# Where the gate columns and the key columns of the retention group stand in a diffusion layer's order of stages

## The chip, the cores and the metric

The kernel runs on 1 core of one Trainium2 chip. The metric is device time in microseconds (us) of one execution, lower is better. A core has five engines, each with a queue of its own that it works off in the order in which the program put it there: TensorE (PE, matrix products; the profile shows its weight loads apart as PEld), VectorE (DVE), ScalarE (ACT), GpSimd (POOL) and SyncE (SP, which here only issues transfers). ACT and POOL issue transfers too.

## The reference, cut to what matters

One layer over 1024 latent tokens and 256 context tokens of width 1024. All tokens go through one input projection, whose columns feed two groups of four heads: a gated delta rule (A) and retention (B).

```python
p = concat([h_ctx, h_lat]) @ w_in                       # 1280 x 4112
qkv_a, z, ab, rq, rk, rv, rg = split(p)                 # 1536, 512, 16, 512, 512, 512, 512 columns
q, k, v = split(short_conv(qkv_a))                      # A: 5 taps along the tokens, then silu
q, k = l2_normalize(q) * HEAD_DIM ** -0.5, l2_normalize(k)
o_gdn = rms_norm(o_f + o_b) * silu(z)                   # o_f, o_b: gated_delta_rule, both directions
rq, rk = apply_rope(rq), apply_rope(rk) * HEAD_DIM ** -0.5
o_ret = head_group_norm(r_f + r_b) * silu(rg)           # r_f, r_b: retention, both directions
y = concat([o_gdn, o_ret])
x = x + g1 * (y @ w_out)
x = x + g2 * swiglu(modulate(rms_norm(x), sh2, sc2))    # 1024 -> 2 x 2816 -> 1024
```

The delta rule needs, for each chunk of tokens and each direction, the inverse of a triangular matrix made from k; then a scan runs over the chunks. The retention is a second scan, which needs rq, rk and rv of a chunk.

## The kernel before, in words

Every large product is made from split float32 values: an operand x becomes hi (rounded by ACT, L319) and lo = x - hi (DVE or POOL, L320), and hi*hi + hi*lo + lo*hi are three matmuls.

- **Norm and modulation** (up to L309) leave the activations of all 1280 tokens in SBUF as `hhi` and `hlo`, transposed, where they stay until the last projection is done.
- **`token_major(g, tiles, finish, store, pl, q)`** (L371) projects 256 columns: group g of the weights is loaded and split in two halves, then each tile of 128 tokens takes 24 matmuls of 256 columns into a PSUM bank `tm` (three banks), `finish` takes the bank to the tile `res`, and `store`'s queue writes `res` to memory. Groups 0 and 1 are rv, 2 and 3 rk, 4 and 5 rq, 6 and 7 rg (the gate), 8 and 9 z. rv and rk run over 10 tiles, the others over 8. `finish` is one ACT instruction for rv, rg and z; for rk and rq it is `fin_rope` (L393): `ra` (L398) and two halves of `res` (L401) on DVE, two POOL instructions (L403), and the store (L391) on POOL's queue, with two buffers of `res`.
- **`conv_block(b, y, lat)`** (L475) projects 128 columns of q, k or v of the delta rule for all tokens (PSUM tile `b2`, `b` in the profile), runs the five taps (ACT L488, DVE L494) and the silu. For k, `kstat` transposes it and makes scales; `ada_rest` puts a column block of the conditioning on DVE (L336) beside it.
- **`pre(t)`** (L568) prepares chunk t of 128 tokens: k times k (`kk`), the transposed q (`qt`), k times q (`kq`), all in three PSUM banks of tag `pb` that are taken in turn; then for each direction the decay matrix `e` from a loaded row `gw` (POOL L591, L593, ACT L595), the tile `ut` (DVE L603), and for latent chunks `sp` (DVE L605, ACT L608, POOL L609). Two buffers each of `gw`, `e`, `ut`, `sp`.
- **`invert(b)`** (L616) inverts 32 x 32 blocks of a batch of chunks by 31 pairs of small DVE instructions (`tmp`, `X`: L638, L640), **`merge(b)`** (L664) puts the blocks together (PE tiles `m`), through the tile `U`, of which there is one buffer. The batches are [0,1,2,9], [3,8,4,7] and [5,6].
- **The scans**: `step(s, d)` (L766; matmuls kS, Tr, up, o) is one step of the delta rule in direction d. `rstate` (L884; matmul `ru`) and `forward` are the retention. A small chain of constants (`rdl`, `lg`, `Z`, from L857) stands ahead of the first `ru`; its tiles lie where `hhi` lay, so it begins once the last projection is done.
- Output projection, feed-forward and final norm follow; they begin at about 720 us of the span.

The code is written in the order norm, rv, k convolutions, q convolutions, rg, chunks of batches 0 and 1 with their inversions, v convolutions, chunks of batch 2, merges, z, first two scan steps, rk, rq, the rest of the scans. This order is only a priority. A scheduler that orders by its own cost estimate fixes each engine's queue when the kernel is built: where it thinks that the next instruction of a higher priority isn't ready, it puts a later one there. So matmuls of a projection stand between those of other stages as filling. On the chip the queues are worked off in that fixed order.

A pool's memory is reused tile by tile: `pre`'s tiles (pool `gp`) lie where the pools `w2` and `r2` were, which `token_major` for rg and `ada_rest` used.

Of the kernel before, what the change touches and what calls it, by code (L numbers as in the profile page):

```python
# [8 lines left out]
F32 = mybir.dt.float32  # L9
# [8 lines left out]
P = 128  # L18
# [5 lines left out]
TT = NTOK // P  # L24
# [13 lines left out]
def build(nc, tc, ap, dbg=None, stop=None, marks=None):  # L38
    root = ExitStack()
    V, S, G, T, SY = nc.vector, nc.scalar, nc.gpsimd, nc.tensor, nc.sync  # L40

    def pool(name, bufs=1, side=None, space=None):
        kw = {}
        if side is not None:
            kw["side"] = side
        if space is not None:
            kw["space"] = space
        if space is not DRAM:
            kw["reuse_waits"] = "tile"
        es = ExitStack()  # L50
        p = es.enter_context(tc.tile_pool(name=name, bufs=bufs, **kw))
        root.push(es)
        p_close[id(p)] = es
        return p
# [3 lines left out]
    def close(p):  # L58
        p_close.pop(id(p)).close()
# [5 lines left out]
    def checkpoint(name):  # L65
        if dbg is not None:
            marks.append((name, int(nc.cur_bb.bb.instructions[-1].name.split("-")[-1])))
        if stop == name:
            raise Stop()
# [91 lines left out]
    try:  # L161
# [13 lines left out]
        W = pool("w", bufs=2)  # L175
# [79 lines left out]
        W2 = pool("w2", bufs=2)  # L255
# [69 lines left out]
        def ada_rest(c, half):  # L325

            c0 = c * D + half * 512
            acc = R2.tile([P, 512], F32, tag="acc", name="acc", bufs=1)
            for k in range(KT):
                if k % 2 == 0:  # L330
                    w = R2.tile([P, 2, 512], F32, tag="adaw2", name="adaw2", bufs=2)
                    SY.dma_start(w, ap["ada_w"][k * P:(k + 2) * P, c0:c0 + 512].rearrange("(a p) n -> p a n", p=P))
                if k == 0:
                    V.tensor_scalar(acc, w[:, 0], csl[:, k, 0:1], None, ALU.mult)
                else:
                    V.scalar_tensor_tensor(acc, w[:, k % 2], csl[:, k, 0:1], acc, ALU.mult, ALU.add)  # L336
            ps = bank_b("gr")
            if c in (2, 5):
                row = R2.tile([1, 512], F32, tag="row", name="row", bufs=1)
                SY.dma_start(row, ap["adarow"][c0:c0 + 512].unsqueeze(0))  # L340
                T.matmul(ps[:1, :], ones[:, 0:1], acc, start=True, stop=True)
                V.tensor_tensor(row, row, ps[:1, :], ALU.add)
                SY.dma_start(grow[0 if c == 2 else 1][:, half * 512:(half + 1) * 512], row)
            else:
                for k in range(4):
                    T.matmul(ps[:, 2 * k:2 * k + 2], acc[:, k * P:(k + 1) * P], ones[:, 0:2], start=True, stop=True)
                ks = slice(half * 4, half * 4 + 4)
                o = ada2[:, c - 3, ks]
                V.tensor_tensor(o, ps[:, 0:8].rearrange("p (k t) -> p k t", t=2)[:, :, 0],
                                adab[:, 8 * c + 4 * half:8 * c + 4 * half + 4], ALU.add)  # L350
                if c == 4:
                    V.scalar_tensor_tensor(o, o, 1.0, gffn[:, ks], ALU.add, ALU.mult)
# [18 lines left out]
        def token_major(g, tiles, finish, store, pl, q=S):  # L371

            w = [weights(ap["wt"][g, :, 4 * kh:4 * kh + 4, :], [4, 256], V, pl, q, raws.get((g, kh)), g == 0)
                 for kh in range(2)]
            c0 = (g % 2) * 256
            for t in tiles:
                tsl = slice(t * P, (t + 1) * P)
                o = bank_a("tm")[:, 0:WIDE if g == 0 else 256]
                for k in range(KT):
                    whi, wlo = w[k // 4]  # L380
                    T.matmul(o, hhi[:, k, tsl], whi[:, k % 4, :], start=(k == 0), stop=False)  # L381
                    T.matmul(o, hhi[:, k, tsl], wlo[:, k % 4, :], start=False, stop=False)  # L382
                    T.matmul(o, hlo[:, k, tsl], whi[:, k % 4, :], start=False, stop=(k == KT - 1))  # L383
                early = pl is W2 or g == 0
                res = (W2 if early else R1).tile([P, 256], F32, tag="res", name="res", bufs=4 if early else 2)
                finish(t, o[:, 0:256], res)
                if g == 0:
                    S.activation(xa[:, t, :], o[:, 256:WIDE], AF.Copy)
                nm = GROUPS[g // 2]
                dst = zd[t - 2, :, c0:c0 + 256] if nm == "z" else rd[t, :, RD[nm], c0:c0 + 256]  # L390
                store.dma_start(dst, res)  # L391
# [19 lines left out]
        LAT, ALL = list(range(2, TT)), list(range(2, TT)) + [0, 1]  # L411
        for g in range(2):
            token_major(g, ALL, fin_copy, S, W if g == 0 else W2)
            ada_rest(2, g)
        checkpoint("rv")


# [52 lines left out]
        V.tensor_copy(gT, ps[:80, :P])  # L470
        SY.dma_start(grow_d, gT)
        close(AB)
        CV = pool("cv", side="right")

        def conv_block(b, y, lat):  # L475

            whi, wlo = weights(ap["wg"][b], [KT, P], G if b % 2 else V, W, SY if b in (4, 5) else S)
            u = CV.tile([P, NTOK], F32, tag="u", name="u", bufs=2)
            for c0, n in (CHUNKS[1:] if lat else CHUNKS):
# [19 lines left out]
        def newy():  # L499
            return CV.tile([P, NTOK], F32, tag="y", name="y", bufs=3)  # L500

# [43 lines left out]
        for h in range(H):  # L545
            y = newy()
            conv_block(h, y, True)
            if h < 2:
                ada_rest(5, h)
            S.dma_start(qd[:, :, h, :].rearrange("t p j -> p t j"),  # L550
                        y[:, NCTX:].rearrange("p (t j) -> p t j", j=P))

        checkpoint("q")
        for g in (6, 7):
            token_major(g, LAT, fin_gate, S, W2, SY)
        checkpoint("rg")
        close(R2)
        close(W2)
        GP = pool("gp")
# [153 lines left out]
        def solve(b):  # L713
            for t in BATCH[b]:
                pre(t)
            checkpoint("pre%d" % b)
            invert(b)
            checkpoint("inv%d" % b)

        solve(0)  # L720
        solve(1)
        for h in range(H):
            y = newy()
            conv_block(8 + h, y, False)
            for t0, n in ((0, 2), (2, 4), (6, 4)):
                ps = bank_b("vT")
                for t in range(t0, t0 + n):
                    T.transpose(ps[:, (t - t0) * P:(t - t0 + 1) * P], y[:, t * P:(t + 1) * P], ident)
                vt = CV.tile([P, 4, P], F32, tag="vt", name="vt", bufs=1)
                for t in range(n):  # L730
                    S.activation(vt[:, t], ps[:, t * P:(t + 1) * P], AF.Copy, scale=sv3[:, t0 + t, h:h + 1])
                S.dma_start(vd[t0:t0 + n, :, h, :].rearrange("t p j -> p t j"), vt[:, :n])
        close(CV)
        checkpoint("v")
        RP = pool("rp", side="right")
        rope = RP.tile([P, TT, P], F32, tag="rope", name="rope")
        GM = pool("gm")
        for t in BATCH[2]:
            pre(t)
        checkpoint("pre2")  # L740
        merge(0)
        SY.dma_start(rope, ap["rope"])
        invert(2)
        checkpoint("inv2")
        merge(1)
# [97 lines left out]
        for s in range(NS0):  # L843
            steps(s)
        checkpoint("scan0")
        for g in (2, 3):
            token_major(g, ALL, fin_rope, G, W)
        for g in (4, 5):
            token_major(g, LAT, fin_rope, G, W)
        close(R1)  # L850
# [118 lines left out]
        close(SC)  # L969
        close(RP)  # L970
        close(GS)
# [524 lines left out]
```

## Time and profile before

| What | Value |
|---|---|
| Device time, median of 3 runs | 1504.32 us (1503.76 to 1508.56) |
| The profiled execution | 1499.94 us; its span, from the first to the last instruction, is 1498.2 us |
| Mean granted TensorE clock | 0.974 of full speed |
| Busy in the span | PE 1405.7 us (94%), DVE 978.5 us (65%), POOL 638.6 us (43%), ACT 607.0 us (41%) |
| Chain that ended last | PE 64%, DVE 12%, DMA 10%, POOL 5%, issue 4%, ACT 3% |

Busy time of an engine is the time in which at least one of its instructions ran. A wait is put down to the instruction that ended it. The rows of the trace name a line of the kernel, an engine, an operation, output<-input, a count, then busy time, mean duration in ns, and the idle time of the engine just ahead of them with what ended it.

### The profile page before, as it was taken

How to read it: one execution, taken by the hardware profiler on the slowest of the kernel's cores; microseconds unless marked ns; L12 is line 12 of the kernel's file. 1: busy time of each engine (PE TensorE's matmuls, PEld its weight loads, DVE VectorE, ACT ScalarE, POOL GpSimd, SP SyncE). 2: the span in 40 equal slices, each digit the busy share in tenths (PEclk: the TensorE clock that was granted, in tenths of full speed). 3: DMA queues.
4: the chain of work that ended last, by engine and by line, in shares of the span. 5: the costliest groups of instructions: out<-in, count | busy, mean ns of one | idle time of the engine just before them, and what ended most of it. 6: DMA issues, size and time to landing. Idle time of an engine off the chain costs nothing.

```text
span 1498.2 us, 24215 instructions
## 1 busy us (share of the span) xinstructions
PE 1405.7 (94%) x8927; PEld 1210.8 (81%) x8927; DVE 978.5 (65%) x1926; ACT 607.0 (41%) x1267; POOL 638.6 (43%) x589
## 2 busy tenths in 40 slices
PE   6899999987898899998799899989999999999997
PEld 2898888976888899988678688878888888788886
DVE  5966695279778345678767786646555555658477
ACT  5733653365451121235544433223333333445445
POOL 0310101387124243224326578989555553325322
PEclk9899999997999999999999999999999999999999
DMA  8555685478597756985742256665222231785863
GB/s 329 197 175 164 207 239 167 143 234 267 147 276 213 227 170 252 370 334 204 246 147 106 86 191 223 240 238 204 105 106 106 106 141 68 237 281 188 295 217 113
DMA packets 171703, 298.16 MB, mean 199 GB/s; under 512 B 43368, under 2 KB 93752, under 8 KB 166208
## 3 DMA queue, kind: packets, MB, share of 16 engines
q1 hardware_dynamic: 119424, 251.07, 48.9%
q10 hardware_dynamic: 49360, 36.88, 8.0%
q0 software_dynamic: 2800, 8.65, 1.6%
q8 instruction: 70, 1.15, 0.3%
q14 instruction: 49, 0.40, 0.1%
HBM read 206.60 MB, written 89.96 MB: 198 GB/s over the span
## 4 chain that ended last, share of the span: by engine, by line
PE 64%; DVE 12%; DMA 10%; POOL 5%; issue 4%; ACT 3%; SPq 1%; ACTq 0%; POOLq 0%; DVEq 0%
PE ffn L1187 8%; PE ffn L1186 8%; PE ffn L1185 8%; PE tm L383 4%; PE tm L382 4%; PE tm L381 4%; PE fo L1313 3%; PE fo L1312 3%; PE fo L1311 3%; PE b L484 2%; PE b L486 2%; PE b L485 2%; PE op L1044 2%; PE op L1046 2%; PE op L1045 2%
## 5 line engine op out<-in xcount | busy, mean ns | idle before, releaser
L381 PE MATMUL tm<-whi,hhi 128*128 128x256 f32 (+1 forms) x704 | 203.9, 292 | 8.7 <-ACT whi L319 4.3
L382 PE MATMUL tm<-wlo,hhi 128*128 128x256 f32 (+1 forms) x704 | 204.5, 292 | 3.1 <-DVE wlo L320 3.1
L383 PE MATMUL tm<-whi,hlo 128*128 128x256 f32 (+1 forms) x704 | 204.4, 293 | 0.0
L381 PEld LDWEIGHTS tm<-whi,hhi 128*128 128x128 f32 x704 | 137.4, 196 | 11.1 <-ACT whi L319 5.4
L382 PEld LDWEIGHTS tm<-wlo,hhi 128*128 128x128 f32 x704 | 138.0, 196 | 5.8 <-DVE wlo L320 3.6
L1185 PE MATMUL ffn<-t,whi 128*128 128x512 f32 x352 | 137.7, 392 | 4.0 <-ACT whi L319 3.0
L383 PEld LDWEIGHTS tm<-whi,hlo 128*128 128x128 f32 x704 | 137.6, 196 | 2.2 <-issue 0.9
L1187 PE MATMUL ffn<-t,wlo 128*128 128x512 f32 x352 | 137.5, 392 | 1.1 <-DVE wlo L320 1.1
L1186 PE MATMUL ffn<-t,whi 128*128 128x512 f32 x352 | 137.8, 392 | 0.5 <-DVE t L1080 0.5
L319 ACT ACTIVATE whi<-wraw 128x512 fp32r<-128x512 f32 (+2 forms) x98 | 75.2, 772 | 132.0 <-PE ffn L1186 77.6
L320 DVE TENSOR_TENSOR wlo<-ws,whi 128x512 fp32r<-128x512 f32 x88 | 94.4, 1073 | 50.1 <-ACT whi L319 50.0
L319 ACT ACTIVATE whi<-ws 128x512 fp32r<-128x512 f32 x88 | 55.6, 631 | 170.6 <-PE ffn L1186 120.1
L320 DVE TENSOR_TENSOR wlo<-wraw,whi 128x512 fp32r<-128x512 f32 (+2 forms) x92 | 100.5, 1094 | 35.6 <-ACT whi L319 35.3
L1312 PE MATMUL fo<-wlo,ahi 128*128 128x512 f32 x308 | 120.0, 390 | 0.8 <-DVE wlo L320 0.8
L1311 PE MATMUL fo<-whi,ahi 128*128 128x512 f32 x308 | 119.3, 390 | 0.7 <-ACT ahi L319 0.7
L1313 PE MATMUL fo<-whi,alo 128*128 128x512 f32 x308 | 118.8, 389 | 0.0
L1185 PE MATMUL ffn<-b,whi 128*128 128x512 f32 x264 | 103.7, 393 | 3.8 <-ACT whi L319 3.8
L1187 PE MATMUL ffn<-b,wlo 128*128 128x512 f32 x264 | 103.7, 393 | 1.6 <-DVE wlo L320 1.6
L1186 PE MATMUL ffn<-b,whi 128*128 128x512 f32 x264 | 103.5, 392 | 0.0
L484 PE MATMUL b<-hhi,whi 128*128 128x512 f32 (+1 forms) x256 | 95.5, 373 | 2.2 <-ACT y L488 2.2
L485 PE MATMUL b<-hlo,whi 128*128 128x512 f32 (+1 forms) x256 | 95.1, 372 | 0.0
L486 PE MATMUL b<-hhi,wlo 128*128 128x512 f32 (+1 forms) x256 | 94.8, 370 | 0.0
(422 smaller groups left out, 3495.3 us busy)
## 6 DMA issues: line engine op xcount, KB each, us to landing
adaw<-ada_w SPq DMA_DIRECT2D x48, 512.0 KB, 5.6
pk<-sd SPq DMA_DIRECT2D x16, 1536.0 KB, 9.7
wraw<-wfi SPq DMA_DIRECT2D x44, 512.0 KB, 3.5
ar<-ad SPq DMA_DIRECT2D x33, 512.0 KB, 6.5
w<-wfo SPq DMA_DIRECT2D x22, 512.0 KB, 3.5
wd<-tw SPq DMA_DIRECT2D x11, 1024.0 KB, 4.8
ad<-act SPq DMA_DIRECT2D x20, 512.0 KB, 4.7
raw<-wd SPq DMA_DIRECT2D x20, 512.0 KB, 5.0
```

Of the source, the lines that this page charges most:

```text
L319: S.activation(hi, raw, AF.Copy)
L320: e.tensor_tensor(lo, raw, hi.bitcast(F32), ALU.subtract)
L381: T.matmul(o, hhi[:, k, tsl], whi[:, k % 4, :], start=(k == 0), stop=False)
L382: T.matmul(o, hhi[:, k, tsl], wlo[:, k % 4, :], start=False, stop=False)
L383: T.matmul(o, hlo[:, k, tsl], whi[:, k % 4, :], start=False, stop=(k == KT - 1))
L484: T.matmul(o, whi[:, k, :], hh, start=(k == 0), stop=False)
L1185: T.matmul(o, whi[:, k, :], xhi(xn, slice(0, 4), k), start=(first and k == 0), stop=False, **kw)
L1186: T.matmul(o, whi[:, k, :], xlo(xn, slice(0, 4), k), start=False, stop=False, **kw)
L1187: T.matmul(o, wlo[:, k, :], xhi(xn, slice(0, 4), k), start=False, stop=(k == 3), **kw)
L1311: T.matmul(po[g][i], ahi[:, ts], whi, start=(j == 0 and not kw), stop=False, **kw)
L1312: T.matmul(po[g][i], ahi[:, ts], wlo, start=False, stop=False, **kw)
L1313: T.matmul(po[g][i], alo[:, ts], whi, start=False, stop=(j == FH - 1), **kw)
```

## The change

Two projections are written at other places. rg (groups 6 and 7) moves from behind the q convolutions to just behind rv. rk (groups 2 and 3) moves from behind the first two scan steps to between the preparation of batch 0 and that of batch 1; the table `rope` that it needs, with its pool, moves ahead of the convolutions' pool and is loaded ahead of `pre`. With this, rg's group 6 takes its weights from pool `w` in place of `w2`, and `res` of groups 0, 1, 6 and 7 has four buffers.

```diff
-                early = pl is W2 or g == 0
+                early = g in (0, 1, 6, 7)
                 res = (W2 if early else R1).tile([P, 256], F32, tag="res", name="res", bufs=4 if early else 2)
...
         for g in range(2):
             token_major(g, ALL, fin_copy, S, W if g == 0 else W2)
             ada_rest(2, g)
+        for g in (6, 7):
+            token_major(g, LAT, fin_gate, S, W if g == 6 else W2, SY)
         checkpoint("rv")
...
         close(AB)
+        RP = pool("rp", side="right")
+        rope = RP.tile([P, TT, P], F32, tag="rope", name="rope")
         CV = pool("cv", side="right")
...
+        SY.dma_start(rope, ap["rope"])
         checkpoint("q")
-        for g in (6, 7):
-            token_major(g, LAT, fin_gate, S, W2, SY)
-        checkpoint("rg")
         close(R2)
         close(W2)
...
         solve(0)
+        for g in (2, 3):
+            token_major(g, ALL, fin_rope, G, W)
         solve(1)
...
-        RP = pool("rp", side="right")
-        rope = RP.tile([P, TT, P], F32, tag="rope", name="rope")
         GM = pool("gm")
...
         merge(0)
-        SY.dma_start(rope, ap["rope"])
         invert(2)
...
         checkpoint("scan0")
-        for g in (2, 3):
-            token_major(g, ALL, fin_rope, G, W)
         for g in (4, 5):
             token_major(g, LAT, fin_rope, G, W)
```

How the queues change is shown at three places. Lines of the kernel after are numbered two higher than before in `pre`, `invert` and `merge`, one higher in `step`, and one lower from the retention on.

First place: PE's queue around the first chunk's `kk`. Before, it stands in the convolution of v (tile `b2_3662`), behind all of rg:

```order
L486 MATMUL b2_3662<-hhi_80,wlo_3602 128x512
L484 MATMUL b2_3662<-hhi_80,whi_3601 128x512
L573 MATMUL kk_2860<-kc_2858 128x128 x4
L485 MATMUL b2_3662<-hlo_81,whi_3601 128x512
L486 MATMUL b2_3662<-hhi_80,wlo_3602 128x512
L484 MATMUL b2_3662<-hhi_80,whi_3601 128x512
L573 MATMUL kk_2901<-kc_2899 128x128 x4
```

After, it stands behind the last `ada_rest` (`gr`) and among the tiles of rk (`tm_3379` is the sixth of twenty):

```order
L383 MATMUL tm_3379<-whi_3208,hlo_81 128x256
L341 MATMUL gr_2705<-acc_2688,ones_67 1x512
L575 MATMUL kk_2865<-kc_2863 128x128 x4
L575 MATMUL kk_2906<-kc_2904 128x128 x4
L381 MATMUL tm_3412<-whi_3202,hhi_80 128x256
L382 MATMUL tm_3412<-wlo_3203,hhi_80 128x256
L383 MATMUL tm_3412<-whi_3202,hlo_81 128x256
```

The chunks' products have moved out of v's convolutions and into rk; the convolutions of v stand behind rk now.

Second place: POOL's queue at chunk 2, the first that has `sp` (`e_2965` and `e_2990` before, `e_2970` and `e_2995` after are its two directions). Before:

```order
L591 TENSOR_SCALAR e_2965<-gw_2963,nG_1279 128x128 x4
L593 AFFINE_SELECT e_2965<-e_2965 128x512
L609 TENSOR_TENSOR sp_2974<-gw_2963,qc_2947 128x512
L591 TENSOR_SCALAR e_2990<-gw_2988,nG_1279 128x128 x4
L593 AFFINE_SELECT e_2990<-e_2990 128x512
L609 TENSOR_TENSOR sp_2999<-gw_2988,qc_2947 128x512
```

After:

```order
L593 TENSOR_SCALAR e_2970<-gw_2968,nG_1751 128x128 x4
L593 TENSOR_SCALAR e_2995<-gw_2993,nG_1751 128x128 x4
L403 TENSOR_TENSOR res_3470<-ra_3471,res_3470 128x2x64 x2
L595 AFFINE_SELECT e_2970<-e_2970 128x512
L403 TENSOR_TENSOR res_3503<-ra_3504,res_3503 128x2x64 x2
L595 AFFINE_SELECT e_2995<-e_2995 128x512
L611 TENSOR_TENSOR sp_2979<-gw_2968,qc_2952 128x512
L391 DMA rd_635<-res_3470 128x256
L391 DMA rd_635<-res_3503 128x256
L611 TENSOR_TENSOR sp_3004<-gw_2993,qc_2952 128x512
```

The rotated keys and their stores stand between a chunk's `e` and its selection, and each of them waits for DVE.

Third place: PE's queue at the last projection tile, `tm_6820`. Before, it ends among the scan's third step (`kS_6922` to `o_6988`), and the first `ru` comes 31 matmuls behind the last row shown here:

```order
L382 MATMUL tm_6820<-wlo_6584,hhi_80 128x256
L383 MATMUL tm_6820<-whi_6583,hlo_81 128x256
L784 MATMUL kS_6922<-S0_5602,pk0_6920 128x128 x2
L784 MATMUL kS_6934<-S1_5612,pk1_6932 128x128 x4
L792 MATMUL Tr_6944<-r_6927,pk0_6920 128x128 x4
L792 MATMUL Tr_6951<-r_6939,pk1_6932 128x128 x4
L799 MATMUL up_6958<-vn_6949,pk0_6920 128x128 x4
```

After, the whole last merge (`U2`) follows it, then the first step's product in one direction, and at once the first `ru`:

```order
L383 MATMUL tm_6820<-whi_6583,hlo_81 128x256
L681 MATMUL m1_5596<-t64_5586,U2_5584 32x32 x32
L688 MATMUL m1_5631<-U2_5584,xt1_5629 32x32
L691 MATMUL m1_5632<-xt1_5629,U2_5584 32x32
L688 MATMUL m1_5631<-U2_5584,xt1_5629 32x32
L691 MATMUL m1_5632<-xt1_5629,U2_5584 32x32 x15
L688 MATMUL m1_5631<-U2_5584,xt1_5629 32x32 x30
L704 MATMUL m2_5687<-t64_5586,U2_5584 64x64 x16
L708 MATMUL m2_5688<-U2_5584,xt2_5689 64x64 x16
L793 MATMUL Tr_6215<-pk0_6211 128x128 x4
L889 MATMUL ru_7002<-pk_6998,kz_7000 128x128 x4
```

The first scan steps and the last merge no longer stand among projection tiles: the steps stand among the `ru`, the merge alone.

## The prediction

> **What bounds the kernel now.** First the page: how much of the span is TensorE's.
>
> ```profile
> span 1498.2 us, 24215 instructions
> PE 1405.7 (94%) x8927; PEld 1210.8 (81%) x8927; DVE 978.5 (65%) x1926; ACT 607.0 (41%) x1267; POOL 638.6 (43%) x589
> ```
>
> PE is busy 94%. The change moves matmuls and removes none, so it can only win PE's idle time and the time lost to a lower clock. Second, busy time by stretch (window, length, then busy us of PE, PEld, DVE, ACT, POOL; granted clock; transfers): from the end of rv to the last q convolution; rg alone; batches 0 and 1 with v's convolutions and nine tiles of z, up to the preparation of chunk 5; merges, z, rk and rq; the scans.
>
> ```profile
> 104.00:245.00 141.00, 140.96 (x812) 121.58 (x810) 103.13 (x162) 65.71 (x191) 11.57 (x8) 1.00 0.71 212
> 245.00:287.00 42.00, 41.83 (x310) 39.29 (x311) 6.28 (x9) 11.11 (x21) 3.98 (x10) 1.00 0.30 98
> 287.00:410.00 123.00, 103.94 (x642) 92.29 (x641) 99.22 (x234) 69.82 (x159) 72.65 (x98) 0.90 0.70 217
> 410.00:587.00 177.00, 163.79 (x2254) 158.57 (x2254) 99.66 (x276) 44.66 (x83) 62.74 (x118) 0.95 0.71 222
> 587.00:720.00 133.00, 120.56 (x1027) 117.39 (x1025) 102.76 (x380) 51.90 (x157) 47.67 (x47) 0.99 0.78 296
> ```
>
> PE loses nothing before 287. It idles 19.1 us in 287 to 410, where DVE is busy 99.2 of 123, and 13.2 us in 410 to 587. The clock, 0.90 and 0.95, costs at most 123 x 0.10 + 177 x 0.05 = 21 us more. So 53 us is the ceiling. In the second row, rg runs with DVE busy 6 of 42; after, it runs as alone behind rv, so that idleness of DVE is moved, not used. What is new is rk beside the chunks. Third, the waits of PE in 287 to 410, then in 410 to 587:
>
> ```profile
> PE kk L573 <- ACT qt L580: 4.8, 2, 2.9
> PE vT L728 <- DVE ut L603: 3.4, 1, 3.4
> PE vT L728 <- ACT vt L731: 3.1, 2, 2.4
> ...
> PE m L679 <- issue: 3.4, 1, 3.4
> PE m L689 <- DMA U<-xd: 2.8, 1, 2.8
> PE m L686 <- issue: 2.5, 2, 1.7
> ```
>
> Chunk products and v's transposes wait for a PSUM bank, that is for DVE and ACT; merges wait for U. In the worst forty us DVE is full while PE has 10.6 us idle and a low clock:
>
> ```profile
> 340.00:360.00 20.00, 16.35 (x96) 14.32 (x95) 18.89 (x49) 12.23 (x29) 16.04 (x25) 0.84 0.75 264
> 360.00:380.00 20.00, 13.05 (x60) 10.13 (x59) 19.48 (x46) 10.72 (x24) 9.45 (x14) 0.76 0.71 213
> ```
>
> **The change part by part.** Prices first: a projection tile on PE (33 us of pure rg), and what one tile of rk costs DVE and POOL; then the small DVE groups.
>
> ```profile
> 248.00:281.00 33.00, 33.00 (x269) 32.47 (x268) 4.39 (x6) 6.84 (x15) 0.00 (x0) 1.00 0.34 108
> L398 DVE TENSOR_TENSOR ra<-tm,rope 128x256 f32<-128x256 f32 x35 | 14.7, 420 | 45.3 <-PE tm L383 45.3
> L401 DVE TENSOR_TENSOR res<-tm,rope 128x128 f32<-128x128 f32 x70 | 16.7, 280 | 11.4 <-DMA rd<-res 7.0 <-DMA zd<-res 4.3
> L403 POOL TENSOR_TENSOR res<-ra,res 128x128 f32<-128x128 f32 x70 | 33.4, 494 | 87.0 <-DVE res L401 86.9
> L391 POOL DMA_DIRECT2D rd<-res x34 | 19.1, 562 | 8.9 <-POOL res L403 8.0 <-DMA rd<-res 0.6 <-DMA pk<-sd 0.3
> L638 DVE TENSOR_TENSOR tmp<-L,X 128x31 f32<-128x31 f32 (+23 forms) x93 | 35.0, 376 | 3.2 <-ACT L L631 1.0
> L640 DVE TENSOR_TENSOR X<-X,tmp 128x31 f32<-128x31 f32 (+23 forms) x93 | 38.6, 415 | 2.4
> L494 DVE SCALAR_TENSOR_TENSOR y<-u,cw,y 128x1022 f32<-128x1022 f32 (+3 forms) x80 | 81.9, 1037 | 9.7 <-ACT y L488 9.4
> L320 DVE TENSOR_TENSOR wlo<-wraw,whi 128x512 fp32r<-128x512 f32 (+2 forms) x92 | 100.5, 1094 | 35.6 <-ACT whi L319 35.3
> ```
>
> 33 us for 269 recorded matmuls is 0.12 us each, 24 of them 2.9 us a tile. A tile of rk costs DVE 0.42 + 2 x 0.28 = 0.98 us and POOL 2 x 0.494 + 0.562 = 1.55 us.
>
> *rg behind rv.* 16 x 2.9 = 46 us of PE as before; stores and silu stay on ACT, the loads on SP. It costs nothing where it goes: DVE and POOL have nothing that PE needs, and the weights come two groups ahead, under the group of 23 us between. What it leaves is the cover of the k and q convolutions: 26 matmuls of rg stood among them, 26 x 0.12 = 3.1 us. DVE is busy 103 of 141 us there, so the holes may stay open or close. Bounds 0 and 6 us lost (twice the filling, for the clock); I take two thirds of the filling, **-2**.
>
> *The chunk stage.* Six tiles of rk (17 us) precede the first chunk's product, in place of 64 matmuls of v's convolution (24 of 256 columns at 0.12, 40 of 512 at an estimated 0.24: 12.5 us). From that product to chunk 5's, the queue of PE now holds 14 tiles of rk (40.3 us) and those 12.5 us more, and 108 matmuls of z (13 us) less: 39.8 us more work. By how much is it longer? DVE had 99.2 busy in 123 us. In the queue after stand, up to chunk 5's ut, 14 ra and 30 res (14 x 0.42 + 30 x 0.28 = 14.3 us), 12 tmp and 11 X more of the second inversion (9.1), one more weight split (1.1) and 4 more taps (4.1): 127.8 us. At the share of before (99.2 / 123 = 0.81) that takes 158 us, at that of 340 to 380 (38.4 / 40 = 0.96) 133. PE alone is busy 103.9 + 39.8 = 144 us at this clock, some 12 less at full clock, so 133 is the floor for it too. The chain of each chunk (POOL e, ACT, DVE ut, next bank) has little to fill DVE with at the stage's start, and an inversion and v's taps behind it; I take 0.84, near the whole stage's row: 152 us. That is 29 us longer for 39.8 us more work, **+11**, between +5 (158) and +30 (133). If stores hold res longer than now (7.0 us of DVE's waiting over 34 stores), it falls under that, to -4.
>
> POOL in the same stage: 72.7 busy now, and 14 x 1.55 = 21.7 us more, 94 of 152. It is hidden if it comes where POOL waits.
>
> *Merges, z and rq.* rk's 20 tiles leave, 57.6 us of PE, and some 80 matmuls of the scan stand behind the first ru now. Work that leaves costs and wins nothing by itself; what counts is the idle time. What covered is gone in two places. First, the end: the last tile, the constants of the retention, the first ru.
>
> ```profile
> 587.03 0.28 PE L383 MATMUL tm<-whi,hlo 128*128 128x256 f32 x1
> 589.74 0.17 DVE L861 TENSOR_SCALAR rdl<-rdl 128x8 f32<-128x8 f32 x1 [0.47 <-DMA rdl<-rdl]
> 596.68 1.95 PE L784 MATMUL kS<-S,pk 128*128 128x128 f32 x16
> 598.57 2.08 POOL L886 TENSOR_TENSOR kz<-pk,Z 128x512 f32<-128x512 f32 x2 [8.73 <-ACT Z L882]
> 600.65 1.06 PE L890 MATMUL ru<-pk,kz 128*128 128x128 f32 x8
> ```
>
> 13.6 us pass, which a scan step and more filled. After, only the last merge and one Tr stand there, some 5 us of matmuls; the rest is idle: -8, between -10 and -4 (the merge's own waits lie in it). Second, the merges' own round trip through the one U, by the chain in order of time:
>
> ```profile
> 465.33 5.24 DMA sd<-U
> 470.69 10.05 DMA U<-un
> 484.27 7.49 DMA U<-xd
> ```
>
> 22.8 us of transfers lie between two merges. Between the first merge's last product and the second's first stood 116 matmuls of tiles (14 us), after 137 (16 us): no change. Between the second and the third, whose U is half as large, stood 137 (16 us), after 94 (11 us): by half of the 10 us of U<-un and the rest as above the trip is 18 us, but it begins no later than DVE's third inversion lets it, -3. For it: PE's waits for m of 8.7 us may shrink, because the third inversion no longer shares DVE with rk, which waited 11.3 us for stores (the L401 row); and the clock's loss, at most 177 x 0.05 = 9 us, gets shorter with the stage. I take +8 of these 18. Together **-3**; bounds -12 (none of the relief, and 1 us more of waiting) and +7.
>
> The Trainium skill (TensorE: Matmul & The Clock Gate, What's actually happening) says that the clock halves after at least one idle window of about 3.4 us. Here the longest single wait in 287 to 410 is 3.4 us, yet 360 to 380 stands at 0.76, so the row speaks for many short waits lowering it too. Read strictly, the short waits cost no clock and only the wait at the end does, one window at half rate, 1.7 us: the sum would be 1 us faster in place of 3.
>
> *Scan steps 0 and 1* have lost their tiles and stand among ru. Nothing in the trace shows them so. The nearest row is the scan's stretch, where PE idles 12.4 of 133 us in 7.5 steps, 1.7 us a step; between 0 (ru covers all) and -7 (twice that for both); I take **-3**.
>
> Sum: -2 + 11 - 3 - 3 = **3 us faster**: span 1498.2 to 1495. The execution was 1499.94; the median of the runs shown, 1504.32, is 4.4 above it, and I count from that: **1501 us**. That is inside 0.3% (4.5 us, about what a measurement of this kernel can tell from no change).
>
> **The rivals.**
>
> *Faster: DVE is filled better.* For it: a tile of rk needs little of DVE, and an inversion is always ready. Against: the first three chunks have POOL, ACT and a transfer of gw in their chain. At a share of 0.93, 138 us, the second term is +25 and the sum 17: 1487.
>
> *The idle only moves.* For it: DVE needs 128 us and PE 132 to 144 in one stage, and the end of the projections stands bare. With -9 for the third part the sum is -3: 1507.
>
> *Slower, POOL becomes the bound of the chunk stage.* Its rows now:
>
> ```profile
> L591 POOL TENSOR_SCALAR e<-gw,nG 128x128 f32<-128x128 f32 x64 | 34.9, 561 | 9.1 <-DVE ut L603 5.0 <-DMA gw<-grow_d 2.5 <-ACT qt L580 1.4
> L609 POOL TENSOR_TENSOR sp<-gw,qc 128x512 f32<-128x512 f32 x14 | 18.6, 1330 | 8.0 <-ACT gw L608 7.8
> 300.00:320.00 20.00, 18.61 (x112) 16.13 (x111) 15.38 (x40) 13.38 (x26) 18.29 (x22) 1.00 0.69 222
> 320.00:340.00 20.00, 15.31 (x90) 12.80 (x89) 14.05 (x34) 14.10 (x31) 15.95 (x22) 0.97 0.91 261
> ```
>
> From 300 to 360 POOL is busy 50 of 60 us, and the key's instructions stand in its queue between an e and its selection, each waiting for DVE, which waits for that e. If the 21.7 us come at POOL's share of 0.84 on top, chunk 7 is 26 us later, and the stage, with v's convolutions behind it, 55 us longer instead of 29 if PE finds no other tile, 42 if it finds some for half of it: -2 in place of +11, 10 slower in all: 1514 (and 1527 with the 55). It makes the kernel slower by over 0.3% once the stage takes 160 us.
>
> *Slower by the stores.* rk's stores leave POOL's queue beside a busy DVE. The two engines get in each other's way: four e took 1.41 us with DVE idle, and 2.68 us beside v's taps:
>
> ```profile
> 281.82 1.41 POOL L591 TENSOR_SCALAR e<-gw,nG 128x128 f32<-128x128 f32 x4 [42.01 <-DMA rd<-res]
> 325.00 2.68 POOL L591 TENSOR_SCALAR e<-gw,nG 128x128 f32<-128x128 f32 x4 [0.36 <-DVE ut L603]
> ```
>
> If each of 14 tiles holds res, and with it DVE, for a tap's length, 1.04 us, DVE needs 142 us, 169 at 0.84: -6 in place of +11, 1518. The Trainium skill (SBUF — State Buffer, SBUF: two separate sides) says that DVE and GpSimd lock a shared port pair for a whole instruction, and that a transfer issued from GpSimd can starve for its descriptors. The two rows agree with the lock; no row shows a starved store, 7.0 us over 34 being small.
>
> **How the numbers follow.** The forecast, from 8 us faster to 2 slower, has 0.38: 0.14 faster by over 0.3%, 0.22 within it, 0.02 slower. Better filled 0.27, faster. Idle only moved 0.10: 0.07 within, 0.03 slower. POOL 0.17 and stores 0.08, slower. So faster 0.41, same 0.29, slower 0.30. The forecast's own range is 1496 to 1506. The whole range takes in the other cases: low 1481, at the floor of 133 us; high 1518, the stores' price and past POOL's. What lies beyond, the sum of all lower ends, is under 2 in 10.
>
> **What would show it.** After, the stretch from the first kk to chunk 5's first kk lasts about 152 us (138: better filled; over 160: POOL or stores), with DVE's busy share there near 0.84. DVE's wait for res by rd stays under 0.5 us a tile; if the stores are to blame it is 1 us or more. POOL idles in that stretch some 50 us; if POOL bounds, under 35. Between the last tm and the first ru PE is idle about 9 us. PE waits for m on U about 9 us in all. PE idles no more than 3 us before the sixth rk tile. It is wrong if the first kk comes much later than 292 us (287.4 now + 17 - 12.5), since then a load ahead of it holds SP's queue, or if a merge waits over 10 us.

## The result, and the profile after

The kernel after takes 1510.09 us (median of 19 runs, 1507.33 to 1516.28) against 1500.39 us (19 runs, 1493.93 to 1508.56). The ratio is 1.0066, 95% interval 1.0051 to 1.0081: 10 us slower, where 3 us faster was forecast.

The page's span and busy times: TensorE has the same work, and the span is longer.

```profile
span 1505.8 us, 24183 instructions
PE 1406.0 (93%) x8927; PEld 1216.8 (81%) x8927; DVE 976.3 (65%) x1926; ACT 602.7 (40%) x1263; POOL 631.3 (42%) x589
```

By stretch (window, length, busy us of PE, PEld, DVE, ACT, POOL, then granted clock, transfers). After: up to the first kk, to chunk 5's kk, to the last tile, to the first ru, to the first yT, the first product of the output projection.

```profile
245.00:290.40 45.40, 45.40 (x272) 38.52 (x270) 39.39 (x69) 18.54 (x49) 9.75 (x13) 1.00 0.75 232
290.40:450.90 160.50, 140.87 (x928) 130.35 (x928) 131.16 (x307) 65.52 (x155) 92.34 (x151) 0.93 0.59 186
450.90:575.00 124.10, 106.87 (x1588) 102.52 (x1586) 62.45 (x173) 38.00 (x73) 33.85 (x59) 0.92 0.75 223
575.00:590.00 15.00, 7.75 (x233) 7.17 (x234) 7.16 (x34) 5.97 (x13) 3.02 (x5) 0.76 0.61 169
590.00:749.50 159.50, 139.56 (x1153) 136.31 (x1154) 111.96 (x419) 63.71 (x179) 50.17 (x47) 0.94 0.80 306
```

Before, cut at the same events (the first yT comes at 733.9, not at about 720):

```profile
287.40:409.40 122.00, 102.94 (x635) 91.37 (x634) 99.22 (x234) 69.42 (x158) 72.65 (x98) 0.90 0.71 217
409.40:587.30 177.90, 164.69 (x2263) 159.47 (x2262) 99.66 (x276) 44.66 (x83) 62.83 (x118) 0.95 0.71 221
587.30:600.70 13.40, 12.04 (x100) 11.38 (x99) 11.33 (x50) 4.07 (x8) 4.05 (x6) 1.00 0.80 290
600.70:733.90 133.20, 116.89 (x989) 113.85 (x988) 102.50 (x366) 56.41 (x166) 48.32 (x44) 0.97 0.80 301
```

A stretch has lost what its length grew beyond the work that moved into it, by the queue's counts and the prices of the prediction (0.12 us a matmul of a tile; 12.5 us for the 64 of v's convolution, 24 of them with 256 columns and 40 with 512). A matmul of a scan step is put at 0.22 us: the trace has two rows for each, and eight rows take 0.89 us.

| Stretch | Length, before to after | Work moved in | Lost |
|---|---|---|---|
| to the first kk | 287.4 to 290.4 | 144 of tiles, 64 of v fewer: +4.8 | -1.8 |
| chunks, to chunk 5's kk | 122.0 to 160.5 | 229 of tiles, 64 of v: +40 | -1.5 |
| merges, to the first ru | 191.3 to 139 | 373 of tiles, 83 of steps fewer: -63 | 10.8 |
| scans, to the first yT | 133.2 to 159.7 | 83 of steps: +18 | 8.2 |

So what stands ahead of chunk 5's kk won 3 us and what follows lost 19: the first yT comes 15.6 us later, and the rest of the span, the same code, is 6 us shorter (651.8 for 658.0). How far to trust it: where two kernels have the same queue in a stage, its length repeats within 1 us (chunk stage after and in two variants of it 160.5, 160.0, 159.7). But from the last output projection matmul to the end, the same code took 650.7 to 658.0 us over all profiles here, before's the longest, so a sum over one profile is good to some 8 us.

Which product ends last turned out to matter most. The last merge (m) and the last projection tile (tm), before and then after:

```profile
L706 PE MATMUL m<-U,xt x160: 218/218/267, 456.2 to 547.5; 64*64 64x64 f32 x160
L383 PE MATMUL tm<-whi,hlo x704: 274/282/597, 41.2 to 587.0; 128*128 128x256 f32 x156, 128*128 128x272 f32 x20
```

```profile
L708 PE MATMUL m<-U,xt x160: 218/218/267, 510.1 to 585.8; 64*64 64x64 f32 x160
L383 PE MATMUL tm<-whi,hlo x704: 274/282/592, 40.9 to 574.6; 128*128 128x256 f32 x156, 128*128 128x272 f32 x20
```

Before, tiles ran on for 39.5 us behind the last merge, over the scan's first steps. After, the last merge ends 11.2 us behind the last tile. From the first m (434.7 and 477.8) the merges take 113 and 108 us: moving tiles away made them 5 us shorter, and they start 43 us later: v's convolutions stand behind rk, and their last transposition (vT) comes at 448.3 in place of 403.1.

In PE's queue the scan's steps, but for the first product of one direction, stand behind the last merge in both kernels. The rows of kS, the product that opens every step but the first, before and then after, and after's two stretches from it to the last o and from there to the first yT:

```profile
L784 PE MATMUL kS<-S,pk x144: 270/275/421, 561.0 to 687.6; 128*128 128x128 f32 x144
```

```profile
L785 PE MATMUL kS<-S,pk x144: 275/275/275, 598.3 to 701.6; 128*128 128x128 f32 x144
598.30:711.90 113.60, 111.20 (x978) 109.77 (x977) 75.42 (x293) 38.88 (x107) 33.17 (x31) 1.00 0.85 336
711.90:749.50 37.60, 21.95 (x137) 20.33 (x136) 30.13 (x111) 20.82 (x62) 14.04 (x13) 0.78 0.63 218
```

Before, kS begins 40 us ahead of the first ru, among tiles; after, 8.5 us behind it, and from there on PE is full up to the last o. So with no tiles left, the place of the last merge sets the time of the first kS, and that the time of yT.

### The profile page after: what moved, and what is told of

It reads as the page before. It is cut to its first block, busy times and chain, and to the rows that moved or that the text cites. A ratio compares the mean times of both kernels' runs of the same rounds, so it can differ in the third digit from the quotient of the medians.

```text
span 1505.8 us, 24183 instructions
## 1 busy us (share of the span) xinstructions
PE 1406.0 (93%) x8927; PEld 1216.8 (81%) x8927; DVE 976.3 (65%) x1926; ACT 602.7 (40%) x1263; POOL 631.3 (42%) x589
## 4 chain that ended last, share of the span: by engine, by line
PE 46%; POOL 6%; DMA 3%; DVE 2%; issue 2%; ACT 1%; SPq 0%; POOLq 0%; DVEq 0%; ACTq 0%
PE ffn L1186 6%; PE ffn L1184 6%; PE ffn L1185 6%; PE fo L1312 5%; PE fo L1310 5%; PE fo L1311 5%; DMA wd<-tw 2%; PE op L1043 2%; PE op L1044 2%; PE op L1045 2%; PE ru L889 1%; POOL tw L1238 1%; PE kS L785 1%; PE Tr L793 1%; PE up L800 1%
## 5 line engine op out<-in xcount | busy, mean ns | idle before, releaser
L320 DVE TENSOR_TENSOR wlo<-wraw,whi 128x512 fp32r<-128x512 f32 (+2 forms) x92 | 104.3, 1135 | 38.9 <-ACT whi L319 38.9
```

What stands on the lines that cost most here:

```text
L320: e.tensor_tensor(lo, raw, hi.bitcast(F32), ALU.subtract)
```

## The experiments

Each ratio is to the kernel before, run in turn on the same chip. "Margin" is the last tm minus the last m in the kernel's profile.

| Kernel | Median us | Ratio (95%) | Margin us |
|---|---|---|---|
| rg early alone (e1) | 1507.19 | 1.0023 (1.0000 to 1.0045) | +39.3 |
| rk early alone (e2) | 1520.32 | 1.0108 (1.0076 to 1.0140) | -18.6 |
| after, half of rk early (e3) | 1506.95 | 1.0026 (1.0007 to 1.0045) | +12.5 |
| after, constants early (e4) | 1517.15 | 1.0098 (1.0067 to 1.0128) | -15.0 |
| before, first steps behind rk, rq (e5) | 1501.28 | 0.9987 (0.9973 to 1.0002) | +32.6 |
| z early in rk's place (e6) | 1490.33 | 0.9912 (0.9890 to 0.9934) | +17.7 |
| e3 and constants early (e7) | 1503.96 | 0.9995 (0.9974 to 1.0016) | +12.5 |
| after, yr loads on ACT (e8) | 1512.31 | 1.0056 (1.0034 to 1.0078) | -15.7 |
| after, batch 2 ahead of v (e9) | 1528.07 | 1.0162 (1.0130 to 1.0193) | -13.0 |
| e6, batch 2 ahead of v (e10) | 1508.74 | 1.0042 (1.0021 to 1.0064) | -1.1 |
| e6, constants early (e11) | 1491.40 | 0.9920 (0.9889 to 0.9952) | +17.8 |
| z early, rg behind q (e12) | 1509.70 | 1.0047 (1.0023 to 1.0071) | +39.4 |
| after, other table (e13) | 1509.68 | 1.0069 (1.0046 to 1.0093) | -12.5 |
| e6, yr loads on ACT (e14) | 1495.52 | 0.9965 (0.9942 to 0.9987) | +6.9 |
| after, v ahead of rk (e15) | 1492.70 | 0.9953 (0.9935 to 0.9972) | +7.7 |
| e6, v ahead of z (e16) | 1522.31 | 1.0114 (1.0089 to 1.0140) | -1.1 |
| e1, v ahead of batch 1 (e17) | 1505.32 | 1.0012 (0.9995 to 1.0030) | +8.5 |

**The halves.** e1: only the two rg edits of the change. e2: only the rk and rope edits. e3:

```diff
         solve(0)
-        for g in (2, 3):
+        for g in (2,):
...
         checkpoint("scan0")
+        for g in (3,):
+            token_major(g, ALL, fin_rope, G, W)
```

> Half of the change: the gate columns behind rv, the key columns where they were before. Theory (the loss lies behind the chunk stage, where the key columns are missing as cover): no change from before, within 3 us (1497 to 1503), PE without idle from 104 us to the first kk. Rival (the gate's move costs, since the convolutions of k and q lose their filling): 4 to 10 us slower than before, 1504 to 1510, with idle of PE between 104 us and the first kk.

> The other half: the key columns between the two preparations, the gate columns behind q as before. Theory: the whole loss stays, 8 to 12 us slower than before, 1508 to 1512, with PE idle of some 24 us from chunk 5's first kk to the first ru, and a clock near 0.91 there. Rival (the gate's move costs): within 3 us of before.

> The kernel after with only the first half of the key columns (group 2, 10 tiles) beside the chunks; group 3 (10 tiles, 29 us of PE) stands behind the first two scan steps again. Theory (missing cover behind the chunk stage): at least half of the 10 us comes back, 1500 to 1505, and the scan's first steps stand among tiles again. Rival (POOL or the stores make the chunk stage too long): its length past the work in it shrinks only in the ratio of the tiles that stay in it, 10 for 14, so 3 us come back, 1507.

e1 is 0 to 7 us slower by its interval, which settles neither side, but the rival's place is wrong: PE has no idle time between 104 us and the first kk.

```profile
104.00:291.00 187.00, 187.00 (x1151) 164.58 (x1149) 110.80 (x171) 81.01 (x216) 16.02 (x15) 1.00 0.59 179
```

e2 loses 11 to 21 us, more than the whole change: the loss belongs to rk, and is larger than expected. e3 gives back 6 of after's 10 us by the ratios (its median is the rival's 1507, on a chip on which before took 1502.59): its stretch from chunk 5's kk to the first ru loses nothing (160.7 us), but its scan does, 152.7 us for before's 133.2 with 2 us more work:

```profile
456.10:594.30 138.20, 124.32 (x1921) 118.53 (x1920) 81.60 (x248) 30.89 (x52) 46.67 (x82) 0.96 0.71 226
594.30:747.00 152.70, 126.98 (x1009) 121.39 (x1010) 104.87 (x378) 59.11 (x171) 51.18 (x47) 0.93 0.75 284
```

**The terms behind the chunk stage, one by one.** e4 and e7 work out `rdl`, `lg`, `gch` and `Z` ahead of `merge(2)`, in pool `rp` (e11 the same on e6). e5 sets `NS0 = 0` in the kernel before. e13 changes how many pieces of the retention go with each scan step. e4, e5 and e13:

```diff
         merge(1)
+        rdl = RP.tile([P, 8], F32, tag="rdl", name="rdl")
+        SY.dma_start(rdl, ap["rdl"].partition_broadcast(P))
...
+        lg = softplus(RP, rdl, 8, "lg")
...
+        S.activation(Z, Z, AF.Exp)
         merge(2)
...
-        NS0 = 2
+        NS0 = 0
...
-        for s, n in enumerate((0,0,3,3,3,2,2,2,2,3)):
+        for s, n in enumerate((0,0,2,2,2,2,2,3,3,4)):
```

> The kernel after with the small constants of the retention (rdl, lg, gch, Z) worked out ahead of the last merge, in a pool that is free then, in place of behind the last projection. Theory (the bare end of the projections is one of the places of the loss: 7.3 us of PE idle between 575 and 590, clock 0.76): idle there falls to some 4 us, 3 to 5 us faster than after, 1505 to 1507. Rival (the last merge's own round trips set that stretch, the constants lie beside them): no change from after, 1509 to 1511.

> The kernel before with one edit: the first two scan steps are written behind rk and rq (NS0 = 0), so that they have no projection tiles around them, as in the kernel after; nothing else moves. Theory (part of the loss is in the scan, which has to take the two steps in): 5 to 10 us slower than before, 1506 to 1512, and the stretch from the first ru to the first yT grows by some 8 us more than the work that moved into it. Rival (bare steps cost nothing, the whole loss is the missing cover of the merges): within 3 us of before.

> The kernel with half of rk early (1506.95 us) and the small constants of the retention worked out ahead of the last merge. Theory (with half of rk back the merges are covered again, and what it still loses is in the scan, where the first ru comes 18 us after the last tile and six forward pieces are left bare at the end): the first ru comes some 8 us earlier, 5 to 10 us faster than with half of rk alone, 1497 to 1502. Rival (the end of the scan is set by the gates on DVE): no change, 1505 to 1509.

> The kernel after with another share of the retention's twenty pieces over the ten scan steps, (0,0,2,2,2,2,2,3,3,4) in place of (0,0,3,3,3,2,2,2,2,3); PE's queue changes at the end of the scan alone, where two forward pieces instead of three follow the last o. Theory (after, the steps of the delta rule and their gates end last, the retention is done before them, and PE waits 6.2 us for yt<-dy): pieces left for the end would fill that wait, but the scheduler moved them the other way, so no gain, 1508 to 1512, and the wait for yt grows to 8 us or more. Rival (the retention's pieces ahead of the last gates delay them): 1503 to 1507.

e4's bare end did shrink, 15.0 to 11.5 us with 6.3 in place of 7.3 idle, and the first ru came 2.3 us earlier; but the kernel was no faster, against both expectations. Its last m came 5.4 us later and with it its first kS (605.5 for 598.3), so that the stretch from the first ru grew by 7 us:

```profile
576.00:587.50 11.50, 5.24 (x197) 4.74 (x196) 4.08 (x14) 4.16 (x8) 2.60 (x5) 0.67 0.76 232
587.50:754.20 166.70, 141.62 (x1193) 139.36 (x1193) 110.06 (x420) 64.83 (x184) 50.20 (x47) 0.91 0.79 296
```

e5 cost nothing, but its steps did not become bare: with merges that end 32.6 us ahead of the last tile, the queue still has most of the two steps' matmuls ahead of the first ru. So it refutes the order in the code as a cause, not bare steps. e7 wins 3 to 5 us on e3 (the intervals just overlap), with a first ru 1.4 us later, not 8 us earlier: the theory's way is not shown, and less came of it than it said. e13 changes nothing, as its theory said, with a wait for yt of 6.8 us (after 6.2, expected 8 or more).

**The chunk stage.** In after's stage the longest wait was one link of four engines. Rows by time (start, length, instruction, in brackets the idle time and what ended it) of SP, POOL and DVE, and PE's wait in 340 to 360:

```profile
335.56 4.32 SPq L626 DMA_DIRECT2D yr<-un  x4
...
341.18 1.51 SPq L588 DMA_DIRECT2D gw<-grow_d  x2
```

```profile
347.69 1.42 POOL L593 TENSOR_SCALAR e<-gw,nG 128x128 f32<-128x128 f32 x4 [7.48 <-DMA gw<-grow_d]
```

```profile
350.35 0.42 DVE L398 TENSOR_TENSOR ra<-tm,rope 128x256 f32<-128x256 f32 x1 [3.01 <-POOL res L403]
```

```profile
PE tm L381 <- DVE res L401: 6.0, 1, 6.0
```

The inversion's loads stand ahead of gw on SP, POOL's e waits for gw, the key's res stands behind e, DVE's ra behind res, and PE's next tile behind DVE. e6 puts tiles there that only ACT finishes, e8 moves the loads (e14 on e6):

```diff
         solve(0)
-        for g in (2, 3):
-            token_major(g, ALL, fin_rope, G, W)
+        for g in (8, 9):
+            token_major(g, LAT, fin_gate, S, W)
...
-                SY.dma_start(yr[k:2 * nb:4].rearrange("r (i j) -> r i j", j=32),
+                S.dma_start(yr[k:2 * nb:4].rearrange("r (i j) -> r i j", j=32),
```

(The first hunk is e6, with z taken from behind the merges and rk put behind the first steps; the second is e8.)

> The kernel after with z (groups 8 and 9, finished by ACT alone) in the place of rk between the two preparations, and rk (finished by DVE and POOL) back behind the first two scan steps. Theory (the chunk stage kept its idle time because the tiles of rk hang on the same DVE and POOL queues as the chunks: in one place POOL waits 7.5 us for gw, res stands behind it, and PE waits 6.0 us for a bank): idle of PE in the chunk stage falls from 19.6 to 12 us or less, and the merges keep rk as cover, 1490 to 1497. Rival (the holes are those of the chunks' own chain, and tiles of any kind only lengthen the stage): idle stays near 19, 1500 to 1506.

> The kernel after with the inversion's four loads yr<-un issued from ACT's queue in place of SP's, where they stand ahead of the next chunk's gw (4.3 us of issuing). Theory (that delay of gw holds POOL, res behind it, and through DVE the banks of rk): PE's wait of 6.0 us for res near 348 us goes, idle in 340 to 360 falls from 8.6 to 4 us or less, 3 to 5 us faster than after, 1505 to 1507. Rival (another link of the chain takes its place): no change from after, 1509 to 1511.

> The kernel with z between the preparations (1490.33 us), and the inversions' loads yr<-un on ACT's queue. Theory (gw no longer waits behind them on SP, worth 5 us in the chunk stage with rk there, but z's tiles don't hang on POOL): at most 2 us in the chunk stage, 1487 to 1491. Rival (the delay of gw holds the chunks themselves): 1483 to 1487.

e6's chunk stage is 22.5 us longer than before's for 160 tile and 64 v matmuls more (31.7 us): 9 us won against 1.5 with rk. Its idle time, 16.1 us, did not fall to 12: PE waited 0.9 us for DVE's res in place of 8.3, and longer for ACT. e8's stage lasts 155.0 us with the same work as after, 5.5 shorter, idle in 340 to 360 6.3 us:

```profile
288.30:432.80 144.50, 128.44 (x858) 117.12 (x858) 105.14 (x242) 88.32 (x177) 72.75 (x110) 0.96 0.65 199
```

```profile
291.20:446.20 155.00, 137.89 (x927) 126.47 (x927) 127.89 (x302) 65.11 (x154) 89.69 (x151) 0.96 0.62 192
340.00:360.00 20.00, 13.69 (x96) 12.87 (x95) 16.42 (x46) 6.45 (x18) 13.13 (x25) 0.83 0.79 248
575.80:747.00 171.20, 141.78 (x1192) 137.99 (x1192) 112.71 (x421) 64.49 (x182) 50.77 (x47) 0.94 0.77 287
```

Its first ru came at 575.8, 14 us ahead of after's, and its first yT at 747.0, 2.5 ahead: the scan took 171.2 us. Its last m came only 6.8 us earlier (579.0) and its first kS 4.3 (594.0). So the gain of the chunk stage was real and was given back behind it, and e8 as a whole is no faster than after. e14 lost 0.5% on e6, against both expectations; its margin is 11 us smaller.

**Where the merges end.** e9 and e10 write `solve(2)` behind `solve(1)`, ahead of v. e15, e16 and e17 move v's loop and the opening of pool `gm` behind `solve(0)`; in e15 rk, in e16 z stands between it and `solve(1)`, in e17 neither, with rk where it was before and rg early.

```diff
         solve(0)
+        for h in range(H):
+            y = newy()
+            conv_block(8 + h, y, False)
...
+        close(CV)
+        GM = pool("gm")
         for g in (2, 3):
             token_major(g, ALL, fin_rope, G, W)
         solve(1)
-        for h in range(H):
-            y = newy()
-            conv_block(8 + h, y, False)
...
```

(e15.) And e9:

```diff
         solve(1)
+        solve(2)
         for h in range(H):
             y = newy()
...
-        for t in BATCH[2]:
-            pre(t)
         merge(0)
-        invert(2)
         merge(1)
```

> The kernel after with the preparation and the inversion of batch 2 written ahead of the convolutions of v, in place of behind them. In all kernels so far 134 to 148 us pass from the last vT to the last m, whatever tiles stand beside, and the kernels in which the last m comes after the last tm are the slow ones. Theory A (merge 1 is late because its loads of U stand on SP behind the third inversion's stores): the stretch from the last vT to the last m falls by 8 us or more, the last m comes no more than 4 us behind the last tm, 1502 to 1506. Theory B (that stretch is the merges' own round trips through the one U, which can only begin when v's memory is free): it stays at 134 us or more, 1508 to 1512.

> The same edit on the kernel with z between the preparations (1490.33 us). Theory A: the merges end earlier under more tiles, 1484 to 1489. Theory B: no gain, 1489 to 1494, since there the last m already stands 17.7 us ahead of the last tm.

> The kernel after with the convolutions of v ahead of rk and of batch 1, rk still between the two preparations. Theory (the time from v's last transposition through the three merges is fixed, 129 to 148 us in fourteen kernels, and rk in front of v pushed its start and so its end past the last tile): the last m ends 12 us or more ahead of the last tm, the scan's first steps have tiles again, and the 18 us lost behind the chunk stage fall below 8: 1494 to 1502. Rival (what costs is rk's finishing on DVE and POOL beside the chunks): no faster than after, 1508 or more.

> The kernel before with the gate columns early and the convolutions of v ahead of batch 1, rk left where it was. It tells whether the gain of v first with rk early (1492.70 us) is v's move or rk's. Theory (v's move only makes room behind it, and rk beside batch 1 is then paid for in full): 1495 to 1502, at least 3 us slower than with rk early. Rival (v's move is the whole gain): 1489 to 1494.

> Both moves that won by themselves: v ahead of batch 1, and z between the preparations with rk behind the first scan steps. By the order the last merge's last matmuls follow the last tile at once, and the first ru comes right behind them. Theory (what decides is whether the last m comes before the last tm): the last m comes within 3 us of the last tm or behind it, the scan has bare first steps, and the time is 1498 to 1508 although each move alone gave 1490 to 1493. Rival (the gains are those of the chunk stage and add up): 1482 to 1490.

e9 and e10 refute theory A, and do worse than B: batch 2's inversion stands ahead of v's taps on DVE, the last vT comes at 459.8 (after 448.3), and the merges follow. e9's m and tm:

```profile
L708 PE MATMUL m<-U,xt x160: 218/218/363, 508.9 to 596.2; 64*64 64x64 f32 x160
L383 PE MATMUL tm<-whi,hlo x704: 274/282/596, 41.2 to 583.2; 128*128 128x256 f32 x156, 128*128 128x272 f32 x20
```

e15 is the opposite: rk stays beside the chunks, with its DVE and POOL work, and 17 us come back. They lie in the scan: its first ru comes at 591.5 (after 589.8), but its first kS at 576.4 (598.3) and its first yT at 732.2 (749.5). The margin is positive, though 7.7 and not 12 us:

```profile
L708 PE MATMUL m<-U,xt x160: 218/218/267, 479.5 to 566.7; 64*64 64x64 f32 x160
L383 PE MATMUL tm<-whi,hlo x704: 274/282/596, 41.3 to 574.4; 128*128 128x256 f32 x156, 128*128 128x272 f32 x20
```

With e17 this makes a square, all four with rg early: v behind, rk late 1.0023, rk early 1.0066; v first, rk late 1.0012, rk early 0.9953. v's move alone is worth nothing that shows, and rk early costs 0.4% or wins 0.6% according to where v stands (e17 was slower than both of its ranges). e16 was foretold by the rule: two moves that won, put together, let the last merge end behind the last tile again.

```profile
L708 PE MATMUL m<-U,xt x160: 218/218/267, 478.3 to 589.5; 64*64 64x64 f32 x160
L383 PE MATMUL tm<-whi,hlo x704: 274/282/593, 41.2 to 588.4; 128*128 128x256 f32 x156, 128*128 128x272 f32 x20
```

It lost, and by 14 us more than expected; its merges took 137 us from first to last, 102 to 121 in all others, so the fixed length that two expectations state is only a tendency (nor does it start at v's last transposition: in e15 198 us lie between). All eight kernels with a negative margin are slower than before, by 0.4 to 1.6%, and all that are faster have a positive one. In all eight the first kS comes 11 to 20 us behind the last m, the last o 113 to 115 us behind that and the first yT another 34 to 40 us later, wherever the first ru stands. A positive one is not enough: e3 loses in the scan, and e12 has the largest margin and is slow.

> The kernel with z between the preparations, and the small constants of the retention worked out ahead of the last merge. Theory (the first ru, 15 us after the last tile, waits for their chain): it comes some 5 us earlier, 2 to 4 us faster, 1486 to 1489. Rival (scan steps fill that stretch anyway): no change, 1489 to 1492.

> The kernel before with one edit: z (groups 8 and 9) between the two preparations; the gate columns stay behind q. Theory (the gate's move is free, all of the gain is z in the chunk stage): within 3 us of the kernel that has both, 1487 to 1494. Rival (the gate's move pays too, since the first chunks need something other than the gate's tiles ahead of them): 1496 to 1502.

e11 is no faster than e6, as its rival said, though its first ru came 10 us earlier. e12, slower than both expectations, shows the other way to lose: with rg behind q, the queue has no tile at all between chunk 5's kk and the first merge, and PE waits for the first merge's loads:

```profile
432.10:451.50 19.40, 8.94 (x41) 7.69 (x42) 16.21 (x50) 8.18 (x28) 5.52 (x12) 0.59 0.83 256
```

```profile
PE m L679 <- DMA t<-xd: 10.3, 4, 8.9
```

e6 has 108 tile matmuls there. Of all kernels run here, e6 is the fastest, and with e11, e14 and e15 faster than both before and after.

## Why the prediction was wrong

Most of its signs held. First kk 290.4 (292 forecast), PE without idle ahead of it, so the convolutions lost no filling that shows: the term of -2 came out at +2. Between the last tm and the first ru PE was idle for 7.3 us (9). PE's waits at the merges for U and for issue sum to 9.1 us (9), none above 3.3 us. Below, the longest waits of PE from chunk 5's kk to the first ru, a tile's first and then the merges':

```profile
PE tm L381 <- ACT res L409: 8.4, 2, 5.5
PE m L688 <- DMA U<-xd: 5.5, 2, 3.3
PE m L688 <- issue: 2.8, 1, 2.8
```

**The chunk stage, +11, came out at +1.5.** It took 160.5 us for a forecast of 152, with DVE's work as forecast (131.2 for 127.8) at a share of 0.82, not 0.84. The prediction said that over 160 would mean POOL or the stores. It was neither as priced: POOL idled 68 us there (forecast 50), and the stores held DVE 5.3 us over 14 tiles, 0.38 a tile:

```profile
DVE res L401 <- DMA rd<-res: 5.3, 4, 3.7
```

What the step missed is a queue that the change doesn't touch: gw behind yr on SP, which e8's 5.5 us price. The POOL rival had the coupling right (res between an e and its selection) and the amount wrong. This term was mis-sized, but it did not decide the time: e8 shortened the stage by 5.5 us, and its ratio is 1.0056 for after's 1.0066.

**Merges, -3, came out at -11, and this is the step that failed.** It set +8 of relief against the bare end and the shorter cover, from waits that were to shrink. They did not: PE's waits for m were 10.9 us for before's 10.4 (8.7 in the three rows that it shows), banks of z waited for ACT (8.4 us above), and the clock stood at 0.92 for 0.95. (The 11.3 us of stores that it set against this are those of rq's tiles too.) The step looked at each place where cover was lost by itself and never asked whether the merges still end under tiles, for which its trace had the numbers: 39.5 us of tiles ran behind the last m, and 57.6 us were to be taken away, 13 of them made up by z. Their difference is an estimate, -18 without z and -5 with it; the margin was -11.2, in e2 -18.6.

**The scan, -3, came out at -8**, in e2, e4, e8 and e9 still more. When the last merge ends behind the tiles, the first steps come into the scan: in the eight kernels where that is so it lasts 156 to 172 us, in the others 133 to 153 (after has 18 us more work in it than before). The prediction priced two steps without tiles and did not ask when the first of them can start. That is the same mistake: the first kS follows the last m, 148 to 154 us pass from it to yT in the eight, and the 7.5 to 18.3 us by which the first ru comes ahead of it make up the rest of the scan.

Of the rivals, the one by which the idle only moves came nearest, with -9 for the third part and 1507 us; it had a chance of 0.10. (The low end of the range, 1481, is 1482 by its own terms.)

Shown by runs: that rk's move carries the loss (e2), that rk beside the chunks wins some 9 us when the merges end under tiles (e15 with e17), that the chunk stage wins 9 us with tiles that ACT finishes (e6), and that with a negative margin yT goes with the last m and the first kS, not with the first ru (e4, e8). Open: why 11 to 20 us pass between the last m and the first kS, and why the merges of e16 take so long.

## What to carry over

Before filling an early stage with work taken from a later one, find the longest chain in the later stage that goes on at its own pace (here three merges, 102 to 121 us mostly), and subtract: if the last of it ends behind the last filler, the gain of the early stage is paid back and more. The subtraction is rough, and the chain's own start and length count too: e10 and e16 move the same tiles as e6, whose margin is 17.7 us, and their merges end 1.1 us behind the last tile. Prefer as filling what only an idle engine finishes: a tile that needs DVE and POOL waits with their queues. A move that wins alone may lose beside another that wins, so the margin is counted anew for each order.

## What the runs showed of the hardware

In this trace the clock's loss comes behind the idle time. After, 340 to 360 has 8.6 us of idle time at 0.94, and the next 20 us, with 0.1 idle, stand at 0.89 (0.56 in 360 to 365, 1.00 from there on):

```profile
340.00:360.00 20.00, 11.43 (x90) 11.06 (x89) 14.22 (x44) 4.97 (x13) 12.46 (x25) 0.94 0.67 218
360.00:380.00 20.00, 19.86 (x115) 17.78 (x114) 19.54 (x43) 9.48 (x27) 15.25 (x22) 0.89 0.70 235
```

A few issues on a queue were dear because something stood behind them: four loads took SP 4.32 us to issue, and PE waited 6.0 us at the far end of the link.
